# Loading the gather indices once and turning them in squares of 32, with batch 0 gathered and stored in two pieces

## The chip, the cores and the metric

One core of a Trainium2 chip. The metric is the device time of one execution in microseconds, less is better. Most executions of one kernel agree within about half a microsecond here: the kernel before gave 88.41 to 89.84 over all runs of this study. "Span" is the part of an execution that its trace covers, about 2 us less than its time. PE, DVE, POOL and SP are the tensor, vector, GpSimd and sync engines of the core; the transfers themselves run on 16 DMA engines.

## The reference

```python
batch, seq, dim = 32, 512, 1024        # x: 32 x 512 x 1024 float32
for b in range(batch):                 # indices: 32 x 128, below 512
    result[b] = x[b, indices[b]]       # 128 rows of 4 KB per batch
```

Rows are copied, nothing is computed: 128 rows of 4 KB in and out, 32 times.

## The kernel before

Each batch is one gather (an indirect DMA that POOL issues, one row per partition) and one store (that SP issues). The first five batches (`HEAD`) are gathered as their indices come. From batch 5 on, repeated indices are first found with DVE and PE, each row is fetched once into one of eight ring buffers, and a matmul with a 0/1 matrix spreads the rows over the output block. The parts that matter here:

```python
    first = const.tile([N, 1], indices.dtype, name="first")          # batch 0's indices, one per partition
    nc.sync.dma_start(out=first[:], in_=indices.rearrange("b n -> n b")[:, 0:1])
    vals = const.tile([B, N], indices.dtype, name="vals")            # all indices, one batch per partition
    nc.sync.dma_start(out=vals[:], in_=indices)
    ...                                                              # iotas on POOL, constants on DVE
    dve(v.tensor_copy, out=vf[:B], in_=vals[:]...[:, :, 0])          # as fp16
    tr = psm.tile([N, B], F32, name="pos")
    pe(mm, tr[:], lhsT=vf[:], rhs=ident[:], start=True, stop=True)   # turned by a matmul
    idxT = const.tile([N, B], I32, name="idxT")
    dve(v.tensor_copy, out=idxT[:], in_=tr[:])                       # one column per batch
    ...
    for b in range(HEAD):
        gather(blocks[b], first[...] if b == 0 else idxT[:, b:b + 1], b)
        store(b)
```

## Time and profile before

| | before |
|---|---|
| time, median of 3 (lowest, highest) | 89.02 us (88.86, 89.25) |
| the profiled execution | 89.52 us, span 87.5 us |
| bytes read and written | 16.81 and 16.78 MB |
| rate in the middle | 412 to 421 GB/s |
| first gather leaves POOL (POOL begins to issue it) / first gathered packet | 2.79 / 4.60 us |
| gather of batch 1 leaves POOL | 4.68 us |

How to read it: for nearly its whole length the kernel is bound by its transfers, so I read the head alone, by the effective start that the prediction defines. Lines of instructions give start and length in us, engine, source line, what was done to which tile, and in brackets how long the engine had been idle before and what ended that.

### The profile page before, as it was taken

What the parts mean: (1) busy time and instruction counts of PE and PEld (TensorE: products, weight loads), DVE (VectorE), ACT (ScalarE), POOL (GpSimd) and SP (SyncE); (2) the same over time, 40 slices, a digit from 0 to 9 for tenths busy, and PEclk for the clock granted to TensorE, in tenths of its full rate; (3) what the DMA queues carried; (4) which work ended last, traced back from release to release, by engine and by line L of the source; (5) the groups of instructions that cost most, each with busy time, mean ns of one, the idle gap of its engine ahead of it and who ended that gap; (6) DMA issues with size and microseconds to landing.
All of it is one profiled execution on the core that took longest, in us unless ns stands there. A gap on an engine that the chain in (4) does not pass through costs nothing.

```text
span 87.5 us, 931 instructions
## 1 busy us (share of the span) xinstructions
PE 58.3 (67%) x184; PEld 23.8 (27%) x184; DVE 41.8 (48%) x265; ACT 40.5 (46%) x63; POOL 33.6 (38%) x46
## 2 busy tenths in 40 slices
PE   0141302006999999999999999998878888885000
PEld 0121101003334343434343433333333332221000
DVE  2399944520497979797979797862000000000000
ACT  6999400000365655555565655554544445555000
POOL 7677787780054545454544444444400000000000
PEclk9999999999999999999999999999999999999995
DMA  0088999999999999999999999999999999999960
GB/s 0 15 223 200 257 352 403 419 419 419 419 416 418 419 421 419 418 418 418 419 414 418 418 412 419 418 418 419 418 419 419 418 419 419 419 419 419 419 251 6
DMA packets 9413, 32.11 MB, mean 367 GB/s; under 512 B 1559, under 2 KB 1591, under 8 KB 9408
## 3 DMA queue, kind: packets, MB, share of 16 engines
q1 hardware_dynamic: 4800, 16.81, 47.2%
q0 software_dynamic: 4608, 15.24, 45.5%
q14 instruction: 4, 0.03, 0.1%
q8 instruction: 1, 0.02, 0.1%
HBM read 16.81 MB, written 16.78 MB: 384 GB/s over the span
## 4 chain that ended last, share of the span: by engine, by line
PE 29%; DVE 29%; DMA 22%; issue 5%; another core or an unknown queue 4%; POOL 1%; ACT 1%; SPq 0%; POOLq 0%; DVEq 0%
PE ps L24 25%; DMA u<-in_x_dram,at 19%; DVE junk L24 5%; DVE s L24 3%; DVE pack L24 3%; DVE s L207 3%; DMA vals<-in_indices_dram 3%; DVE junk L188 3%; DVE lead L24 2%; DVE nth L24 2%; PE pos L24 2%; DVE slot L24 2%; DVE pack L200 1%; DVE atF L204 1%
## 5 line engine op out<-in xcount | busy, mean ns | idle before, releaser
L24 PE MATMUL ps<-u,s 128*128 128x512 f32 x108 | 53.9, 626 | 3.6 <-DMA u<-in_x_dram,at 3.6
L226 ACT COPY block<-ps 128x512 f32<-128x512 f32 x54 | 31.6, 585 | 39.4 <-PE ps L24 31.1
L110 POOL DMA_INDIRECT u<-in_x_dram,at x27 | 26.9, 997 | 26.2 <-PE rk L24 13.0
L24 PEld LDWEIGHTS ps<-u,s 128*128 128x128 f32 x108 | 18.8, 194 | 29.1 <-issue 16.0
L24 DVE SCALAR_TENSOR_TENSOR junk<-bc,idxF,below 128x128 f16<-128x128 f32 x18 | 6.3, 350 | 3.3 <-PE rk L24 3.3
L218 ACT COPY u<-zero 128x1024 f32<-128x1024 f32 x8 | 7.7, 1040 | 0.0
L24 DVE TENSOR_SCALAR s<-bc,atF 128x128 f32<-128x128 f32 x18 | 6.3, 351 | 0.6
L24 PE MATMUL rk<-lead,above 128*128 128x1 f16 x18 | 2.9, 163 | 5.2 <-DVE junk L24 5.2
L24 DVE TENSOR_SCALAR lead<-cnt 128x1 f16<-128x1 f32 (+1 forms) x36 | 3.9, 150 | 4.6 <-remote 4.1
L24 DVE TENSOR_SCALAR pack<-turn,slot,lead 128x128 f16<-128x128 f16 x18 | 5.7, 315 | 0.7
L202 PE MATMUL pos<-near,pack 128*128 128x1 f16 x9 | 1.4, 181 | 5.9 <-DVE pack L200 4.3
L110 POOL DMA_INDIRECT block<-in_x_dram,idxT x4 | 3.8, 946 | 1.7 <-issue 0.9
L24 PEld LDWEIGHTS <-pack 128*128 128x128 f16 x18 | 1.7, 96 | 9.2 <-DVE pack L24 8.8
L24 PE MATMUL bc<-vf,ident 128*128 128x128 f16 x18 | 3.9, 227 | 0.0
L24 PE MATMUL pos<-near,pack 128*128 128x1 f16 x18 | 3.1, 172 | 0.9
L202 PEld LDWEIGHTS <-pack 128*128 128x128 f16 x9 | 0.8, 104 | 9.0 <-DVE pack L200 4.4
L200 DVE TENSOR_SCALAR pack<-turn,slot,lead 128x128 f16<-128x128 f16 x9 | 2.3, 320 | 2.0 <-remote 2.0
L24 DVE TENSOR_TENSOR nth<-nth,shift 128x1 int32<-128x1 int32 x18 | 2.9, 159 | 0.6
L24 DVE CAST slot<-nth 128x1 f32<-128x1 int32 x18 | 2.8, 154 | 0.6
L24 DVE TENSOR_SCALAR at<-pos 128x1 int32<-128x1 f32 x18 | 2.7, 149 | 0.8 <-PE pos L24 0.5
L207 DVE TENSOR_SCALAR s<-bc,atF 128x128 f32<-128x128 f32 x9 | 2.6, 345 | 0.9 <-DVE atF L204 0.9
L188 DVE SCALAR_TENSOR_TENSOR junk<-bc,idxF,below 128x128 f16<-128x128 f32 x9 | 3.0, 345 | 0.0
(37 smaller groups left out, 24.0 us busy)
## 6 DMA issues: line engine op xcount, KB each, us to landing
out_dram<-block SPq DMA_DIRECT2D x32, 512.0 KB
u<-in_x_dram,at POOLq DMA_INDIRECT x27
block<-in_x_dram,idxT POOLq DMA_INDIRECT x4
vals<-in_indices_dram SPq DMA_DIRECT2D x1, 32.0 KB
first<-in_indices_dram SPq DMA_DIRECT2D x1, 1.0 KB
block<-in_x_dram,first POOLq DMA_INDIRECT x1
```

What stands on the lines that cost most here:

```text
L24: self.last = do(*args, **kw)
L110: nc.gpsimd.indirect_dma_start(out=dst[:], out_offset=None, in_=xf[:], in_offset=bass.IndirectOffsetOnAxis(ap=at, axis=0), element_offset= ...
L188: v.scalar_tensor_tensor(out=junk[:], in0=bc[:, b - g0], scalar=idxF[:, col(b)], in1=below[:], op0=ALU.is_equal, op1=ALU.mult, accum_out=c ...
L200: v.tensor_scalar(out=pack[:], in0=turn[:], scalar1=slot[:, col(b)], scalar2=lead[:, col(b)], op0=ALU.is_equal, op1=ALU.mult)
L202: pe.last = mm(pos[:, b - g0:b - g0 + 1], lhsT=pack[:], rhs=near[:, col(b)], start=True, stop=True)
L204: v.tensor_scalar(out=t[:, w], in0=pos[:, :n], scalar1=float(FAR), scalar2=None, op0=ALU.add)
L207: dve.last = v.tensor_scalar(out=s[:], in0=bc[:, b - g0], scalar1=atF[:, col(b)], scalar2=None, op0=ALU.is_equal)
L218: nc.scalar.copy(out=u[:], in_=zero[:].to_broadcast([N, D]))
L226: nc.scalar.copy(out=blocks[b][:, w], in_=ps[:])
```

## The change

It takes away batch 0's own index load, and with it the second small transfer at the start. All indices are loaded once and turned on DVE, in squares of 32 x 32, without PE. To let the stores begin early, batch 0 is gathered as two pieces of 64 rows, each stored as soon as it has landed. The second piece needs its 64 indices from partition 0 on, hence two more squares into `half`.

```diff
-    first = const.tile([N, 1], indices.dtype, name="first")
-    nc.sync.dma_start(out=first[:], in_=indices.rearrange("b n -> n b")[:, 0:1])
     vals = const.tile([B, N], indices.dtype, name="vals")
     nc.sync.dma_start(out=vals[:], in_=indices)
 ...
-    tr = psm.tile([N, B], F32, name="pos")
-    pe(mm, tr[:], lhsT=vf[:], rhs=ident[:], start=True, stop=True)
+    low = vals[:].bitcast(I32).rearrange("p (n two) -> p n two", two=2)[:, :, 0]
     idxT = const.tile([N, B], I32, name="idxT")
-    dve(v.tensor_copy, out=idxT[:], in_=tr[:])
+    for n in range(0, N, B):
+        dve(v.transpose, out=idxT[n:n + B], in_=low[:, n:n + B])
+    half = const.tile([N // 2, B], I32, name="half")
+    for n in range(0, N // 2, B):
+        dve(v.transpose, out=half[n:n + B], in_=low[:, N // 2 + n:N // 2 + n + B])
+    dve(v.tensor_copy, out=vf[:B], in_=low)
 ...
-    for b in range(HEAD):
-        gather(blocks[b], first[:].bitcast(I32)[:, 0:1] if b == 0 else idxT[:, b:b + 1], b)
+    h = N // 2
+    gather(blocks[0][:h], idxT[:h, 0:1], 0)
+    store(0, 0, h)
+    gather(blocks[0][h:], half[:, 0:1], 0)
+    store(0, h, h)
+    for b in range(1, HEAD):
+        gather(blocks[b][:], idxT[:, b:b + 1], b)
         store(b)
```

## The prediction

> **What bounds the kernel now.** I read the busy-by-slice part of the page first, because the traffic is nearly the whole job: rows in, rows out.
>
> ```profile
> PE   0141302006999999999999999998878888885000
> DVE  2399944520497979797979797862000000000000
> DMA  0088999999999999999999999999999999999960
> GB/s 0 15 223 200 257 352 403 419 419 419 419 416 418 419 421 419 418 418 418 419 414 418 418 412 419 418 418 419 418 419 419 418 419 419 419 419 419 419 251 6
> HBM read 16.81 MB, written 16.78 MB: 384 GB/s over the span
> ```
>
> A slice is 2.19 us. From the eighth slice to the thirty-eighth (about 15 to 83 us) the transfers run at 412 to 421 GB/s without a dip; the packet records of the trace show a 4 KB packet taking 159 ns there, so sixteen engines give 16 x 4096 B / 159 ns = 412 GB/s. Slices three to six read 223, 200, 257 and 352 although the DMA row already shows 8 and 9: packets are in flight, but they wait.
>
> The chain that ended last names other things, and I don't follow it:
>
> ```profile
> PE 29%; DVE 29%; DMA 22%; issue 5%; another core or an unknown queue 4%; POOL 1%; ACT 1%; SPq 0%; POOLq 0%; DVEq 0%
> ```
>
> PE and DVE stand there because gather, spread and store pass a ring of eight buffers round between them. But the transfers are full through that whole stretch, and in the tail too: the last gather has landed at 77.97 us and stores alone still fill the engines to 84. A faster PE would only wait for a transfer. So the time is: when the transfers begin, plus what they lose before they are full, plus the bytes at 418 GB/s, plus the ending. The change touches the first two alone. The third view is a table by stretches (columns: stretch, length, busy us of PE, PEld, DVE, ACT, POOL, clock, DMA share, GB/s):
>
> ```profile
> 4.00:5.00 1.00, 1.00 (x10) 0.98 (x11) 0.77 (x6) 1.00 (x3) 0.32 (x1) 1.00 0.62 61
> 5.00:6.00 1.00, 0.30 (x3) 0.00 (x0) 1.00 (x10) 1.00 (x2) 0.70 (x2) 1.00 0.65 225
> 6.00:7.00 1.00, 0.00 (x0) 0.00 (x0) 1.00 (x10) 1.00 (x2) 0.88 (x1) 1.00 1.03 274
> 7.00:8.00 1.00, 0.42 (x3) 0.29 (x4) 1.00 (x9) 1.00 (x2) 0.82 (x1) 1.00 0.53 119
> 8.00:9.00 1.00, 0.00 (x0) 0.00 (x0) 1.00 (x7) 1.00 (x2) 0.69 (x2) 1.00 1.09 311
> 9.00:10.00 1.00, 0.50 (x4) 0.25 (x3) 1.00 (x7) 0.69 (x1) 0.70 (x2) 1.00 0.93 291
> 10.00:11.00 1.00, 0.33 (x2) 0.17 (x2) 0.79 (x7) 0.00 (x0) 0.69 (x2) 1.00 0.94 221
> 11.00:12.00 1.00, 0.00 (x0) 0.00 (x0) 0.96 (x5) 0.00 (x0) 0.99 (x1) 1.00 0.86 291
> 12.00:14.00 2.00, 0.00 (x0) 0.00 (x0) 0.05 (x1) 0.00 (x0) 1.40 (x2) 1.00 1.01 403
> ```
>
> The eight stretches to 12 us moved 61+225+274+119+311+291+221+291 = 1793 KB, which is 4.3 us at 418 GB/s. So by 12 us the kernel stands where one would that began at full rate at 12 - 4.3 = 7.7 us. I call this the effective start; what the change is worth is how far it moves it. Of the 7.7 us, 4.6 pass before the first gathered packet (packet records) and 3.1 are lost after it.
>
> Where the loss comes from, in the packet records: up to 10.16 us only gathers are in flight. The first packets of gathers 0 and 1 take 0.3 to 1.3 us each instead of 159 ns, and those from 8 to 12 us still 240 to 300 ns on average. Once stores flow on all engines (about 12 us) a gather packet takes 159 ns too: a second queue gives the engines something to do while a read is on its way. The stores' own wait and the instructions at the head:
>
> ```profile
> SPq L116 <- DMA block<-in_x_dram,first: 5.9, 1, 5.9
> ...
> 0.74 0.38 SPq L63 DMA_DIRECT2D first<-in_indices_dram  x1
> 1.18 0.41 SPq L65 DMA_DIRECT2D vals<-in_indices_dram  x1
> ...
> 2.79 1.11 POOL L110 DMA_INDIRECT block<-in_x_dram,first  x1 [0.37 <-DMA first<-in_indices_dram]
> 3.64 0.27 DVE L24 CAST vf<-vals 32x128 f16<-32x128 int32 x1 [1.00 <-DMA vals<-in_indices_dram]
> 4.21 0.19 DVE L24 CAST idxT<-pos 128x32 int32<-128x32 f32 x1 [0.30 <-PE pos L21]
> 4.68 0.95 POOL L110 DMA_INDIRECT block<-in_x_dram,idxT  x1 [0.79 <-DVE idxF L24]
> ```
>
> The reader is to see that gather 0 leaves at 2.79 because its indices have a load of their own, gather 1 only at 4.68, behind cast, matmul and copy. The store of batch 0 is issued at 7.48, but its first packet moves at 10.16.
>
> **What the Trainium skill says.** "DMA: Bandwidth & Descriptors", section "Queues, rings and completion order": each engine takes turns between the queues that it has work for, and drains a whole packet of descriptors from one before it switches. The trace agrees in kind: store 0 gets two engines' worth of packets by 11.5 us and the rest after, when 381 gather packets (nearly three gathers) have started. "SBUF — State Buffer", section "Door 1: The DMA port swizzle": 64 adjacent partitions reach 8 of the 16 ports, so half the rate for a single such transfer. No transfer before has 64 partitions, so the trace can't show it. "VectorE: DVE Perf Modes", section "Two Vector instructions with no wait between them": an operation whose output starts in another quadrant than the last one's is held until that one is done. Before, 32-column operations last 0.18 to 0.19 us and start 0.10 apart (idxT, idxF, near); I expect 0.19 apart for the squares, as they go to other quadrants each time.
>
> **The change, part by part.**
> Removed: the load `first` (one issue, 0.44 us of SP's time between the two issues; 128 packets of 8 bytes at 7 to 9 ns, nothing), the transposing matmul and the wait for it (vf to idxT, 3.91 to 4.21: 0.30 us). Added: six squares on DVE, one gather and one store more (32 semaphore packets of 9 ns, nothing). The bytes are the same.
> (1) The load of `vals` moves up 0.44, to 0.74. DVE began 2.46 after the issue before (1.18 to 3.64), so at 3.20 now; DVE is free from 2.63. One of its 32 packets took 0.79 us; without such a one it would be 0.6 earlier.
> (2) Squares: 2 x 0.19 = 0.38 for the rows of the first half, 4 x 0.19 = 0.76 if the gather waits for the whole tile, 1.14 for all six. Then POOL starts 0.18 after DVE's end (idxF ends 4.50, gather 1 starts 4.68). Gather 0a starts at 3.20 + 0.38 + 0.18 = 3.76, or 4.14 with four; I take 3.9, against 2.79: 1.1 later.
> (3) POOL's time for 64 rows isn't in the trace. 128 rows take 0.95, so between 0.5 and 0.95; I take 0.7. 0a ends at 4.6, and 0.71 after the end (3.89 to 4.60 before) its first packet moves: 5.3, against 4.60: 0.7 later. With the 0.30 between issues, 0b runs 4.9 to 5.6 and gather 1 starts at 5.9 instead of 4.68; all later gathers are 1.2 behind.
> (4) Landing of 0a: gather 0 took 2.54 from first to last packet (4.60 to 7.14), of which 8 x 0.159 = 1.27 is moving and 1.27 latency. Half has 4 x 0.159 = 0.64, so 1.9: 7.2. The store leaves 0.34 after (7.14 to 7.48 before): 7.55. So the halving buys back what the later start costs, no more, if the ports don't halve the rate (then 0.6 later).
> (5) What is ahead of the store. An issue on SP shows packets 1.0 later (1.18 to 2.22 for `vals`), so store 0a is ready at about 8.6. Before, at 8.5, gathers 1 and 2 were there already (starts 4.68 and 5.93, plus 1.8). Now gather 1 is (5.9 + 1.8 = 7.7), gather 2 (9.0) is not. So stores flow on most engines after gather 1, which I put at 7.2 + 0.8 for 0b + 2.0 for gather 1 = 10.0, instead of 11.7. By then 256 packets have moved: 256 x 159 ns / 16 = 2.5 us, effective start 10.0 - 2.5 = 7.5, against 7.7.
> (6) Off the path: `vf` is cast after the squares, 3.20 + 1.14 = 4.34 against 3.64, and the first `junk` comes 0.4 to 0.5 later. Gather 5 leaves at about 10.9 now and needs its `at` at 8.4; the ring's backlog covers the rest.
> Sum: -0.2. Since store 0b follows 0a closely and starts the second queue twice, and a load without the slow packet would give more, I shade it to -0.35: 89.02 - 0.35 = 88.67.
>
> **Rivals.** A: the later gathers cost their full 0.7 to 1.1 us and the stores gain nothing, because 64 partitions move at half rate, all four squares are waited for, and POOL takes nearly as long for 64 rows as for 128. For it: the first packet surely comes later. Against: up to 12 us the gathers are slowed by reads on their way, not by issue (1.25 us apart). It makes 89.8. B: the stores start much earlier, at about 8.5 on all engines, and the loss after the first packet halves (3.1 to 1.6): effective start 5.3 + 1.6 = 6.9, so 88.2; without the slow packet 87.6. For it: 159 ns packets wherever two queues run. Against: step 4. C: the head is hidden anyway by the ring's backlog; against it, no later slice has a gap in which a late start could be made up. It makes 89.0.
>
> **Range and chances.** 2% is 1.78 us, so faster needs an effective start below 5.9, only 0.6 after the first packet, less than one cold read; slower needs one above 9.5, beyond A by a microsecond. Eight in ten: 87.7 to 89.8. Chances: faster 0.05, same 0.91, slower 0.04.
>
> **What would show it.** Step 1: first square at 3.2 (2.6 to 3.3). Step 2: starts 0.19 apart, first gather at 3.7 to 4.2. Step 3: its POOL time 0.5 to 0.95, gather 1 at about 5.9. Step 4: store 0a issued near 7.5. Step 5: GB/s in slices four to six above 200, 257, 352, and 400 reached a slice earlier. From 15 us on all rows as before. I am wrong if the stores are issued a microsecond away from 7.5, or if the rate in the middle changes.

## The result, and the profile after

The changed kernel took 90.41 us (median of 4; 90.12 to 90.64) beside 88.95 before: ratio 1.0156, 95% interval 1.0115 to 1.0197. A ratio here is the mean time of one kernel's runs over that of the other's runs of the same rounds, so it isn't quite the ratio of the medians. Executions over 1.5% slower than the fastest of the same kernel are left out of the means. It is slower by about 1.4 us: within 2%, as the most likely class said, but outside the predicted range of 87.7 to 89.8.

The row of the page of the changed kernel that answers to that of before (GB/s; a slice is 2.2 us):

```profile
GB/s 15 0 140 155 348 388 362 368 421 414 421 420 420 416 420 416 421 418 416 418 412 416 420 420 420 418 410 420 414 421 418 420 418 418 418 423 420 418 163 6
```

The middle is as before. In the head the fifth and sixth slices are better (348 and 388 against 257 and 352), but the third and fourth are worse (140 and 155 against 223 and 200), and so are the seventh and eighth (362 and 368 against 403 and 419): the head lasts longer. The same in stretches, first before, then after (last column GB/s; the stretch 12 to 14 of before, at 403, is in the prediction):

```profile
4.00:8.00 4.00, 1.72 (x14) 1.26 (x15) 3.77 (x31) 4.00 (x6) 2.71 (x3) 1.00 0.71 170
8.00:12.00 4.00, 0.83 (x5) 0.42 (x4) 3.75 (x22) 1.70 (x2) 3.08 (x4) 1.00 0.96 279
...
14.00:16.00 2.00, 0.47 (x5) 0.32 (x6) 0.94 (x5) 0.00 (x0) 1.59 (x2) 1.00 1.02 418
16.00:18.00 2.00, 0.00 (x0) 0.00 (x0) 1.13 (x5) 0.00 (x0) 1.49 (x2) 1.00 1.02 418
18.00:20.00 2.00, 0.00 (x0) 0.00 (x0) 0.48 (x4) 0.00 (x0) 1.49 (x2) 1.00 1.02 416
```

```profile
4.00:8.00 4.00, 1.71 (x13) 1.24 (x13) 3.64 (x31) 4.00 (x6) 3.07 (x4) 1.00 0.63 139
8.00:12.00 4.00, 0.91 (x5) 0.42 (x4) 3.72 (x23) 1.69 (x2) 2.90 (x3) 1.00 0.88 307
12.00:14.00 2.00, 0.79 (x5) 0.47 (x6) 1.65 (x9) 0.00 (x0) 1.59 (x2) 1.00 1.00 393
14.00:16.00 2.00, 0.16 (x1) 0.00 (x0) 1.86 (x14) 0.00 (x0) 1.42 (x2) 1.00 1.02 328
16.00:18.00 2.00, 0.00 (x0) 0.00 (x0) 0.33 (x2) 0.00 (x0) 1.66 (x2) 1.00 1.01 399
18.00:20.00 2.00, 0.00 (x0) 0.00 (x0) 0.00 (x0) 0.00 (x0) 1.39 (x3) 1.00 1.02 416
```

By 12 us both have moved the same: 4 x (170 + 279) = 1796 KB before, 4 x (139 + 307) = 1784 KB after. By 20 us the sums are 1796 + 2 x (403 + 418 + 418 + 416) = 5106 KB and 1784 + 2 x (393 + 328 + 399 + 416) = 4856 KB. The difference of 250 KB is 0.6 us at 418 GB/s, and 218 KB of it arise between 14 and 18 us, 171 of them after 15 us (3 x 422 KB before, 3 x 365 after), from where I had said that all rows would be as before. From 20 us on the two run alike until the engines begin to fall empty: the last moment at which eight packets are in flight is 84.50 before and 85.08 after (packet records), again 0.6 us. The rest of the 1.1 us between the two spans is the ending, from there to the last packet: 1.40 before, 1.95 after, but 1.15 in the second trace of the changed kernel. So the ending is scatter, and so is half a microsecond of every single trace; times and intervals decide below, the traces say where to look.

The head's instructions in the changed kernel:

```profile
2.55 0.81 DVE L24 STREAM_TRANSPOSE idxT<-vals 32x32 int32<-32x32 int32 x4
3.19 1.06 POOL L110 DMA_INDIRECT block<-in_x_dram,idxT  x1 [0.77 <-DVE idxT L24]
3.39 0.41 DVE L24 STREAM_TRANSPOSE half<-vals 32x32 int32<-32x32 int32 x2
...
4.55 0.92 POOL L110 DMA_INDIRECT block<-in_x_dram,half  x1 [0.30 <-DVE idxF L24]
...
5.78 0.96 POOL L110 DMA_INDIRECT block<-in_x_dram,idxT  x1 [0.30 <-issue]
```

Two things stand out. The first gather leaves at 3.19 instead of 2.79. And a gather of 64 rows keeps POOL as long as one of 128: 1.06 and 0.92 us, against 1.11 and 0.95 before. Batch 0 therefore costs two issues, and the gather of batch 1 leaves at 5.78 instead of 4.68; all later ones are 1.1 us behind too.

The Trainium skill had this. "DMA: Bandwidth & Descriptors", section "Anatomy of one DMA — SWDGE (gpsimd) path", says of descriptor generation that many descriptors can be emitted before the incremental cost shows. The trace agrees, with 0.92 us for 64 and 0.95 for 128. Its section "Rules for kernel authors" says of two transfers to disjoint partition halves "Don't bother — they serialize". Here too they came one after the other: the second half's first packet started at 6.24 us, the first half's last at 6.21, though the second issue was 1.36 us later in any case. I weighed neither in the prediction.

### The profile page after: what moved, and what is told of

Same layout as the page of the kernel before. It is cut to its first block, busy times and chain, and to the rows that moved or that the text cites.

```text
span 88.6 us, 934 instructions
## 1 busy us (share of the span) xinstructions
PE 60.2 (68%) x183; PEld 24.6 (28%) x183; DVE 43.0 (48%) x270; ACT 40.6 (46%) x63; POOL 34.5 (39%) x47
## 4 chain that ended last, share of the span: by engine, by line
PE 30%; DMA 29%; DVE 25%; issue 4%; POOL 3%; ACT 1%; POOLq 0%
DMA u<-in_x_dram,at 29%; PE ps L24 27%; DVE junk L24 3%; DVE s L24 3%; DVE pack L24 3%; DVE junk L193 3%; DVE nth L24 2%; DVE lead L24 2%; DVE pack L205 2%; PE pos L24 2%; DVE slot L24 1%; POOL rank L74 1%; POOL u L110 1%; DVE at L24 1%; DVE idxT L24 1%
## 5 line engine op out<-in xcount | busy, mean ns | idle before, releaser
L24 PE MATMUL ps<-u,s 128*128 128x512 f32 x108 | 55.4, 641 | 8.5 <-DMA u<-in_x_dram,at 8.4
L24 PEld LDWEIGHTS ps<-u,s 128*128 128x128 f32 x108 | 19.3, 199 | 30.9 <-ACT block L231 13.9
L24 DVE TENSOR_SCALAR s<-bc,atF 128x128 f32<-128x128 f32 x18 | 6.3, 351 | 0.6
L24 DVE TENSOR_SCALAR pack<-turn,slot,lead 128x128 f16<-128x128 f16 x18 | 5.7, 315 | 0.7
L110 POOL DMA_INDIRECT block<-in_x_dram,idxT x5 | 4.9, 971 | 2.0 <-DVE idxT L24 0.8
L190 PE MATMUL bc<-vf,ident 128*128 128x128 f16 x9 | 1.1, 306 | 4.3 <-DVE idxF L24 4.3
L24 PE MATMUL bc<-vf,ident 128*128 128x128 f16 x18 | 4.0, 232 | 0.0
L24 PEld LDWEIGHTS <-ident 128*128 128x128 f16 x18 | 1.8, 102 | 4.2 <-issue 4.2
```

The source lines that it names most:

```text
L24: self.last = do(*args, **kw)
L110: nc.gpsimd.indirect_dma_start(out=dst, out_offset=None, in_=xf[:], in_offset=bass.IndirectOffsetOnAxis(ap=at, axis=0), element_offset=b * ...
L190: mm(bc[:, b - g0], lhsT=ident[:, col(b)].to_broadcast([N, N]), rhs=vf[:], start=True, stop=True)
```

## The experiments

The theories, in the order in which they came:
- Theory 1: the halving is the cause, by way of the second POOL issue.
- Theory 2: the squares and the later index work cost in themselves.
- Theory 3: transfers of 64 rows load the engines unevenly and lengthen the ending.
- Theory 1b, after the first four runs: two causes that add, the later first gather and the second issue, so the schedule of the gathers is everything. Theory 2b is its rival: the index path costs beyond the schedule.
- Theories 4 and 5, on how halving costs: by the POOL issue as such, or by slow first reads that each half meets anew.

Each result is a ratio with its 95% interval, and what it is in microseconds of the 89 before. All results were correct. The edits are shown cut down to what matters.

**The halving undone, the squares kept** (e1).

```diff
-    half = ...                                           # and its two squares
 ...
-    gather(blocks[0][:h], idxT[:h, 0:1], 0); store(0, 0, h)
-    gather(blocks[0][h:], half[:, 0:1], 0);  store(0, h, h)
-    for b in range(1, HEAD):
+    for b in range(HEAD):
```

> The squares stay, batch 0 goes in one gather and one store again. Theory 1 (the halving: a gather of 64 rows takes POOL as long as one of 128, so every later gather and the stores of batches 1 and 2 come 1.1 us later and the stores run dry at 14 to 16 us): gather 1 starts at about 4.6 as before, effective start at 20 us near 8.1 (before 7.9, changed 8.5), time 89.2. Theory 2 (the squares, which delay batch 0's indices by 0.4 us and the rest of the index work): still 90.2. Theory 3 (64-row transfers load the engines unevenly and lengthen the ending, last packet 1.95 us after half of the engines are empty instead of 1.4): the ending goes back to 1.4, effective start stays near 8.5, 89.9.

Measured: 90.21 us, ratio 1.0109 (1.0069 to 1.0150), about +1.0 us. The whole of batch 0 waits for all four squares:

```profile
3.66 1.11 POOL L107 DMA_INDIRECT block<-in_x_dram,idxT  x1 [1.24 <-DVE vf L24]
5.08 0.95 POOL L107 DMA_INDIRECT block<-in_x_dram,idxT  x1 [0.30 <-issue]
```

POOL sat idle for 1.24 us. The bracket names `vf`, but the gather needs `idxT` alone, and POOL started 0.28 us after the last square's end (3.38), as it did after the copy into `idxT` before (4.40 to 4.68). The first gather is 0.87 later than before, batch 1's 0.40. So halving isn't needed for the loss; Theory 1 alone falls. The ending was 1.15 us.

**The halving alone** (e2): the kernel before, with a third small load that brings the second half's 64 indices to partition 0.

```diff
+    half = const.tile([N // 2, 1], indices.dtype, name="half")
+    nc.sync.dma_start(out=half[:], in_=indices.rearrange("b n -> n b")[N // 2:, 0:1])
 ...  # batch 0 in two gathers and two stores, from first[:h] and half
```

> The kernel before with batch 0 in halves alone, the indices of both halves by loads of their own, no squares. Theory 1: gather 1 starts near 5.3 instead of 4.68, effective start at 20 us 8.2 to 8.5, time 89.7 to 90.2. Theory 2: as before, 89.0. Theory 3: effective start as before (7.9), the ending half a us longer, 89.5.

Measured: 89.45 us, ratio 1.0036 (1.0000 to 1.0072), about +0.3 us, with batch 1's gather late again:

```profile
5.34 0.96 POOL L112 DMA_INDIRECT block<-in_x_dram,idxT  x1 [0.30 <-DVE junk L195]
```

The interval just reaches 1: the halving costs little, and it isn't the larger part either. In its trace the early stores did bring a gain, and it was lost again: the effective start (packet records) was 7.35 at 12 us against 7.77 before, and 8.14 at 20 us against 7.88. The ending was 1.09 us, so 64-row transfers needn't lengthen it: Theory 3 falls, although its time, 89.5, is the one measured. (In g4 below, without halves, the ending was 1.86.)

**Gathered in halves, stored in one piece** (e3): `store(0)` after both gathers in place of the two half stores.

> The changed kernel with batch 0 still gathered in halves but stored in one piece, after both have landed. Theory 1: the loss is the gathers'; store 0 goes at about 8.75 instead of 7.32, so it is no better than the change: 90.4 to 90.8. Theory 2: 90.4. Theory 3 (half stores): the ending goes back to 1.4 us, 89.9.

Measured: 90.30 us, ratio 1.0138 (1.0095 to 1.0181), like the change. The early half store, the purpose of the halving, buys nothing that these runs can see.

**Own load for batch 0, squares for the rest** (e4, and again as f4).

```diff
 # the changed kernel, with
+    first = const.tile([N, 1], indices.dtype, name="first")
+    nc.sync.dma_start(out=first[:], in_=indices.rearrange("b n -> n b")[:, 0:1])
 ...
+    gather(blocks[0][:], first[:].bitcast(I32)[:, 0:1], 0)   # whole, no halves
```

> Batch 0's own index load and one gather as before, squares for all other batches in place of the matmul. Theory 1: gather 0 at 2.8, gather 1 at 4.2 (POOL free) instead of 4.68, effective start about 0.2 lower than before: 88.8. Theory 2: the squares cost here too, 89.5 to 90. Theory 3: as before, 89.0.

> Again the own load for batch 0 with squares for the others, in five rounds, as it may beat both kernels: theory 1b, with gather 1 half a us earlier and the first gather unmoved: ratio 0.995 to 1.000.

Measured: 0.9983 (0.9938 to 1.0028), then 1.0006 (0.9959 to 1.0053). The squares cost nothing that shows where the first gather stays put: within these intervals, about 0.4 us to each side, Theory 2 falls for the squares. Batch 1's gather left at 4.16 instead of 4.68, and the time didn't follow; a small cost of the squares could hide behind that, but not in f2 below. Both traces of this kernel (spans 86.9 us) lie among its quicker executions, so I don't read a gain from them. It is a tie with the kernel before, not a better version.

**The change once more** (f1), unedited.

> The changed kernel unedited, for a second trace and a tighter ratio. Theory 1b (two causes that add: every 0.1 us by which the first gather starts later costs 0.1 us, and a second POOL issue for the same rows costs some more): ratio 1.013 to 1.017 again, the ending in the new trace about 1.3 us (last packet after half of the engines are empty) as in the four experiments. Theory 3 (uneven engines): an ending of 1.9 us again.

Measured: 1.0125 (1.0066 to 1.0184), ending 1.15 us. In this trace the head's second dip lies a little earlier:

```profile
12.00:14.00 2.00, 0.79 (x5) 0.47 (x6) 1.65 (x9) 0.00 (x0) 1.59 (x2) 1.00 0.86 307
14.00:16.00 2.00, 0.16 (x1) 0.00 (x0) 1.86 (x14) 0.00 (x0) 1.43 (x2) 1.00 1.03 375
```

The dip is there again, at 307 and 375 GB/s, in another place; the effective start at 20 us is 8.49 as in the first trace (8.48).

**Halves by loads of their own, squares for the rest** (f2): the whole change, but the first gather leaves at 2.76.

> Everything of the change but its index path for batch 0: both halves by loads of their own, so the first gather starts at 2.75 instead of 3.19, squares for the other batches. Theory 1b: 89.4 as the halves alone (e2: 89.45), ratio 1.003 to 1.007. Theory 2 (the squares and the later index work cost in themselves): 90.0 or more.

Measured: 89.54 us, ratio 1.0030 (0.9973 to 1.0087), the same as the halves without squares (e2). The squares are innocent a second time, within the intervals.

**The two index loads exchanged** (f3): in the kernel before, `vals` first and `first` second, so that gather 0 leaves at 3.23 and batch 1's stays at 4.65.

> The kernel before with its two index loads exchanged: batch 0's indices come 0.44 us later, the others' 0.44 earlier. Theory 1b: gather 0 starts at 3.2, gather 1 at 4.6 or so, time 0.4 us longer, ratio 1.004 to 1.006. If the first gather's start does not count but the number of gathers ahead does: 1.000.

Measured: 1.0023 (0.9972 to 1.0073), +0.2 us. The dose of 0.44 us is too small for these intervals: it excludes neither 0 nor 0.44.

**A POOL issue that moves no row** (g1): between the gathers of batches 0 and 1, a gather of 64 rows whose indices are all out of bounds.

```diff
+    far = const.tile([N // 2, 1], I32, name="far")
+    v.memset(far[:], FAR)
+    void = const.tile([N // 2, D], F32, name="void")
 ...
+        if b == 0:
+            gather(void, far[:, 0:1], 0, bounds_check=S - 1, oob_is_err=False)
```

> The kernel before with one gather more on POOL between those of batches 0 and 1, of 64 rows whose indices are all out of bounds, so that it moves no row. Theory 4 (halving costs because of its extra POOL issue: batch 1 and all later gathers leave 1.2 us later): gather 1 at 5.3, ratio 1.003 to 1.008. Theory 5 (halving costs because each half meets the slow first reads anew, POOL's issue is innocent): 1.000.

Measured: 89.86 us, ratio 1.0115 (1.0065 to 1.0164), about +1.0 us, more than either theory had. POOL's instructions of this run, and the stretch behind them:

```profile
2.76 1.11 POOL L110 DMA_INDIRECT block<-in_x_dram,first  x1 [0.34 <-DMA first<-in_indices_dram]
4.17 0.94 POOL L110 DMA_INDIRECT void<-in_x_dram,far  x1 [0.30 <-DVE idxF L24]
5.42 0.96 POOL L110 DMA_INDIRECT block<-in_x_dram,idxT  x1 [0.31 <-DVE lead L196]
```

```profile
12.00:14.00 2.00, 0.79 (x5) 0.47 (x6) 1.68 (x8) 0.00 (x0) 1.70 (x2) 1.00 0.81 217
```

An issue without a single row (it adds 80 packets of 4 bytes, 7 to 9 ns each) takes 0.94 us, puts batch 1's gather at 5.42, and leaves a dip at 217 GB/s: from 12 to 14 us 9 store packets started, against 91 before. So POOL's issue by itself is enough for a loss, and it isn't innocent, as Theory 5 had it. But the other half of Theory 5 is in the packet records: where batch 0 is gathered in halves, 18 to 24 of the second half's 64 packets took over 200 ns (the change, f1, e2, e3, f2, g2); where it is gathered whole, 0 to 3 of the second 64. What the issue and the slow reads are each worth in the halving isn't separated. Why the halving with the same issue loses only 0.3 us is open; that its two issues do carry rows may be the reason, but no run tests it.

**The change's schedule without its index path** (g2): the halves of e2, with the load of all indices in front of the two small ones.

> Halves with loads of their own and no squares, but the load of all indices first: half 0a leaves at about 3.2, 0b at 4.6, batch 1 at 5.85, the changed kernel's own schedule of gathers with none of its index path. Theory 1b (the schedule of the gathers is the whole cause): ratio 1.011 to 1.016 as the change. Theory 2b (squares or the index path cost beyond the schedule): 1.003 to 1.008.

Measured: 89.65 us, ratio 1.0093 (1.0046 to 1.0140), about +0.8 us. The gathers leave when those of the changed kernel do (3.19, 4.55, 5.78), within 0.05 us:

```profile
3.23 1.06 POOL L112 DMA_INDIRECT block<-in_x_dram,first  x1 [0.81 <-DMA first<-in_indices_dram]
4.60 0.92 POOL L112 DMA_INDIRECT block<-in_x_dram,half  x1 [0.30 <-issue]
5.82 0.96 POOL L112 DMA_INDIRECT block<-in_x_dram,idxT  x1 [0.30 <-DVE slot L203]
```

So the schedule alone, with neither squares nor `low`, gives most of the loss, though it lies between what Theory 1b asked (1.011 to 1.016) and what Theory 2b did (1.003 to 1.008). Its interval overlaps those of the change. Whether a remainder of 0.3 to 0.6 us belongs to the index path stays open.

**A large dose** (g3): four more loads of the indices in front, into tiles that nobody reads. And **the schedule of e1 without squares** (g4): one such load between `vals` and `first`.

> The kernel before with four more loads of the indices in front, into tiles that nobody reads: about 1.8 us later for batch 0's indices and everything behind. Theory 1b (a later start is passed on whole): 1.6 to 2.0 us more, ratio 1.018 to 1.023. If part of the start is hidden: under 1.012. If the head's loss grows with it: over 1.025.

> The kernel before with batch 0's index load behind that of all indices and one load more that nobody reads: gather 0 at about 3.7 and gather 1 at about 5.1, the schedule of the whole batch 0 with squares (e1) without squares. Theory 1b: ratio 1.008 to 1.012 as there (1.011). Theory 2b: 1.003 to 1.006.

Measured: g3 1.0227 (1.0181 to 1.0273), +2.0 us for a first gather 1.84 us later and batch 1's 1.37 later; g4 1.0081 (1.0035 to 1.0127), +0.7 us for 0.90 and 0.42. The second is the loss of e1 (1.0109 for 0.87 later) within the intervals, without a square.

All together, by the starts of the first two batches' gathers. The effective start is 20 us less the bytes moved by then (packet records, 4 KB packets alone) at 418 GB/s, in the one traced execution:

| kernel | batch 0 in | gather 0, us | gather of batch 1, us | ratio | effective start, us |
|---|---|---|---|---|---|
| before | one | 2.79 | 4.68 | 1 | 7.88 |
| e4 / f4 | one | 2.75 / 2.79 | 4.16 / 4.20 | 0.9983 / 1.0006 | 7.28 / 7.41 |
| f3 | one | 3.23 | 4.65 | 1.0023 | 7.79 |
| g4 | one | 3.69 | 5.10 | 1.0081 | 8.27 |
| e1 | one | 3.66 | 5.08 | 1.0109 | 8.32 |
| g3 | one | 4.63 | 6.05 | 1.0227 | 9.13 |
| g1 | one, and an empty issue | 2.76 | 5.42 | 1.0115 | 8.24 |
| e2 | halves | 2.75 | 5.34 | 1.0036 | 8.14 |
| f2 | halves | 2.76 | 5.35 | 1.0030 | 8.05 |
| g2 | halves | 3.23 | 5.82 | 1.0093 | 8.59 |
| the change / f1 | halves | 3.19 | 5.78 | 1.0156 / 1.0125 | 8.48 / 8.49 |
| e3 | halves, one store | 3.19 | 5.78 | 1.0138 | 8.81 |

## Why the prediction was wrong

The class was right and the size was not: -0.35 us said, about +1.4 measured. By its steps:

1. **The index load.** Squares were to begin at 3.2; they began at 2.55, as soon as DVE was free, for the load had landed at 2.41, 1.7 us after its issue. The slow packet of the trace before didn't come again. The error was in the change's favour.
2. **The squares.** 0.19 us apart was predicted; they started 0.16 to 0.24 apart, each after the one before had ended, and four took 0.81 us. Right. The first gather waited for two of them and left at 3.19, earlier than the 3.7 to 4.2 I had named.
3. **POOL's time for 64 rows.** I took 0.7 us, from "between 0.5 and 0.95". It was 1.06 and 0.92: no saving. Only by luck, because step 1 erred the other way, did batch 1's gather leave at 5.78, near the 5.9 said.
4. **The landing of the first half.** Store 0a issued at 7.32, 7.55 said (first packet 4.95, 5.3 said). Right, with the same luck.
5. **What is ahead of the store. This is the step that failed.** Its event came as said: the stores flowed sooner, seventeen of their packets having started by 10.49 us (9.79 in the second trace) instead of 11.54. The gain from it didn't. I put the effective start at 7.5 at 10 us, and there it was 7.6 (6 x 167 KB from 4 to 10 us). But I set it against the 7.7 of the kernel before, which is its value at 12 us; at 10 us that kernel stood at 6.9 (6 x 214 KB). So I counted as if the head ended when the stores begin, and nothing were lost after that. At 12 us the effective starts were equal (packet records: 7.77 before, 7.83 and 7.77 after), and at 20 us the changed kernel was behind, 8.48 and 8.49 against 7.88. By 14 us 127 store packets had started before, 127 and 118 after; by 16 us 198 before, 140 and 157 after. The first trace shows where: batch 0's last store packet started at 14.21 (14.14 before), but batch 1's first only at 15.34 (14.35 before). That store needs the rows of batch 1, whose gather is 1.1 us late; it was issued at 11.58 instead of 10.76, and that of batch 2 at 13.48 instead of 12.40. Between 14 and 15.5 us the changed kernel started 2 store packets, the one before 45. The gather packets, again without a second queue beside them, took 201 ns on average there, against 160. That is the dip at 328 GB/s. In the second trace the lull lies elsewhere: 5 store packets from 11 to 12 us, batch 0's last at 15.00, batch 1's first at 15.04. So that the stores fall behind is in both traces; that they do so for want of batch 1's rows is a reading of the first, which no run tests by itself. I had described the effect of a missing second queue for the first gathers, and did not ask whether it would come a second time.
6. **Off the path.** The later `vf` and `junk` did no visible harm: with the same squares and an unmoved first gather (f2, e4) nothing was lost beyond the halving.

Of the signs named for step 5, slices five and six were above those of before, slice four was not (155), and 400 GB/s came in the tenth slice instead of the seventh. Neither sign of being wrong came, so they did not guard against what happened. Three readings in the prediction need correcting. Gather packets from 8 to 12 us took 234 ns on average (210 to 308 by microsecond; four in five took about 159), not 240 to 300. POOL starts 0.28 us after `idxT` is ready, not 0.18 after `idxF`, which it doesn't need. And the store's 16 packets by 11.5 us don't show that engines take turns between queues, because the packet records don't name the engine.

In the sum, then, the term "-0.2 for the stores" should have been the price of the schedule: +0.8 in g2 (0.4 to 1.2), which has it without the squares. It splits into about +0.3 for the halving with its second issue (e2, f2; both intervals reach zero) and about +0.5 for all gathers half a microsecond later, which is the difference of g2 and e2 and no better known than to half a microsecond. The first gather's start alone, in f3, gave +0.2. Of the change's +1.1 to +1.4, the rest is within the intervals but not settled.

Among the rivals, A was nearest (89.8). Of its three reasons one came true, POOL's time; half rate didn't show, and the first gather did not wait for all four squares. What I held against it, that up to 12 us the gathers wait for reads and not for issue, may hold as far as it goes: with g1's empty issue the effective start at 12 us was even better, 7.17 against 7.77. But the late gathers were paid for afterwards, from 12 to 14 us, where I did not look; the empty issue cost 1.0 us (0.6 to 1.5). B's argument, faster packets where two queues run, held in part (178 ns from 10 to 12 us in the changed kernel, beside 61 store packets) and didn't help, since the stores fell behind. The range may have been too narrow for another reason too, which no run tests: I measured the loss against one traced execution at 89.52 us, half a microsecond slower than the median that I subtracted from.

## What to carry to other kernels

Before cutting a gather into pieces, look at what one issue costs whatever its size: here 64 rows took POOL 0.92 us and 128 rows 0.95, so every piece delays the later gathers by a whole issue. In the head of this kernel that cost 1.0 us with an empty issue and about 0.3 with two halves. Follow a head to the point where the rate stays full, not to the point where the second queue starts, and compare two kernels at the same moment: an early store's gain can be lost again while the next stores are waited for. And a small load of its own for the first batch can be worth keeping, since a later start of all gathers was passed on to the end: +2.0 us for 1.84 (first gather) and 1.37 (batch 1).

## What the Trainium skill lacked or had wrong

- "DMA: Bandwidth & Descriptors" calls descriptor generation "small, variable" and gives about 1 us to the first byte on POOL's path, but no time for which one indirect issue keeps POOL, by rows. Here it was 0.92 to 1.06 us for 64 rows, 0.94 to 1.11 for 128, and 0.94 for 64 rows that are all out of bounds, with 0.30 us between two issues: one gather in about 1.25 us. The first packet came 1.8 us after the first issue began (2.79 to 4.60).
- None of the pages that I read says how much slower gathered rows are read while no other queue has work: 4 KB packets of gathers took 234 ns on average at 8 to 12 us in the kernel before, and 159 ns from 20 us on.
- "SBUF — State Buffer", section "Door 1: The DMA port swizzle", lets one expect half rate for 64 partitions. Nothing of the kind showed: the first half's 64 packets in the changed kernel started within 1.26 us, the first 64 of the whole gather before within 1.33, with a median of 159 ns in both. But slow first reads hold up both (21 and 18 packets over 200 ns), so it doesn't test the page's rate for one large transfer.
